# A hybrid encoder layer: input-projection weights split once, stored to DRAM and fetched back for the second half of the tokens

## The chip, the cores and the metric

The kernel runs on one core of one Trainium2 chip. The metric is the device time of one execution in microseconds (us); lower is better.

## The reference, cut to what matters

One layer is computed for 2048 prompt tokens and for 8 sample requests of 16 tokens, which share all weights. Everything is float32.

```python
def layer(x, ...):
    h = rms_norm(x, norm_g[0])
    z = h @ w_in                                   # 1024 -> 3592 columns
    qa, ka, va, qb, kb, vb, ob, ib, fb = split(z)
    att = rms_norm(band_attention(qa, ka, va), g_att)          # 8 heads of 64, band of 9 chunks of 64
    hb = mlstm(qb, kb, vb, ib, fb)                             # 4 heads of 128, state carried along the tokens
    mlstm_out = head_rms_norm(hb) * g_mlstm * sigmoid(ob)
    x = x + rms_norm(concat(att, mlstm_out) @ w_out, norm_g[1])
    x = x + rms_norm(conv_ffn(rms_norm(x, norm_g[2])), norm_g[3])   # 1024 -> 2 x 2816 -> 1024
```

The change concerns `h @ w_in` alone.

## The kernel before, in words

TensorE multiplies in float32r. Each float32 operand is split in two parts, a high part (`h`, a cast on ScalarE) and a low part (`l`, the float32 value less the high part, a subtraction on VectorE), and each product is made of three matmuls (`mm3`, lines 95 to 97: high by high, high by low, low by high).

The tokens are taken in two halves (`HALVES`). In the first are the 8 first tiles of 128 prompt tokens and the sample tile, in the second the 8 last tiles. The columns of `w_in` are cut into 14 groups (`GROUPS`): `va0`, `va1` (values of attention), `qk0` to `qk3` (queries and keys of attention), `qb0` to `qb3` and `vo0` to `vo3` (queries, keys, values and gates of the four mLSTM heads). The list `seq` runs through the 14 groups for the first half and then through the same 14 groups for the second half, so each group's weights are loaded and split twice. A normalised and transposed input (`hT`) of a half stays in SBUF through its 14 groups; `norm_tile` makes it from the rows `xr` (load at line 212, TensorE transposes at line 67 into `hT_pt`).

`load_group` brings the weights of one group, ahead by one group. The tiles `wi_h` and `wi_l` (tags `wh` and `wl`, two buffers each) take the parts. The raw weights come in two pieces `wi_raw` of 512 KB through one buffer (line 1169, issued by SyncE, here SP); each piece is cast and subtracted in two steps (lines 1175 and 1176). The second piece can be loaded only when the first has been split.

Beside the groups run two streams of units, one of attention heads and one of mLSTM heads (`pipes`). `pump` adds up the units' costs of TensorE and VectorE, written in by hand, and takes up to two further units from the streams while VectorE's sum lies below `SHARE` (0.615) of TensorE's. The steps of `load_group` are counted in it: 0.6 us of VectorE for each cast and subtraction. After the last group comes the output projection (`project`, matmuls `wo`), with the rest of the streams beside it, and then the FFN (`ua`, `ub`, `uec`, `dn`, `dnm`).

The order in which the instructions of each engine finally stand is set by a scheduler, which takes the program order as priority and works with its own estimates of durations, so a change in one place moves rows elsewhere. Each engine, SP's list of DMA issues among them, runs its rows strictly in the order that was set. ScalarE (ACT) issues DMAs too: the stores of projected rows (`qTd`, `kTd`, `vd`, `qkbd`, `vobd`). DMA issues also wait, by a semaphore, for earlier DMAs.

Further names in the rows below: `qk_st` is the SBUF copy of a `qk` result (lines 224 and 226) that empties a PSUM bank, of which there are two for these results; `qraw`, `kraw`, `vraw` are attention operands read back; `cs` is the mLSTM state of the samples, `cus` the matmul results on it; `skr`, `svr` are the samples' caches; `whl` is the DRAM tensor that the change adds.

Of the kernel before, what the change touches and what calls it, by code (L numbers as in the profile page):

```python
# [10 lines left out]
F32 = mybir.dt.float32  # L11
F32R = mybir.dt.float32r
# [5 lines left out]
P = 128  # L18
# [26 lines left out]
def hymba_step(ctx: ExitStack, tc: tile.TileContext, I: dict, O: dict):  # L45
    nc = tc.nc

    const = ctx.enter_context(tc.tile_pool(name="const", bufs=1))
    wpool = ctx.enter_context(tc.tile_pool(name="wpool", bufs=1))
    small = ctx.enter_context(tc.tile_pool(name="small", bufs=4))  # L50
    psum = ctx.enter_context(tc.tile_pool(name="psum", bufs=2, space=PSUM))
    dram = ctx.enter_context(tc.tile_pool(name="dram", bufs=1, space=DRAM))
# [10 lines left out]
    def dt_(shape, name):  # L63
        return dram.tile(shape, F32, tag=name, name=name)
# [40 lines left out]
          for p in range(2)]  # L105
    qkbd = [[dt_([P, 2, 512 if s < 4 else 128], f"qkbd{p}_{s}") for s in range(5)] for p in range(4)]
    vobd = [[dt_([P, 4 if s < 4 else 1, 256], f"vobd{p}_{s}") for s in range(5)] for p in range(4)]
    mixd = [dt_([P, 4, D], f"mixd{s}") for s in range(4)]
    mixs = dt_([P, 512], "mixs")
    atts = [dt_([P, 512], f"atts{b}") for b in range(DB)]  # L110
# [131 lines left out]
    def group_T(wh, wl, half, chunks, dsts, scales, name, outs=(None, None)):  # L242
        for c in range(2):
            for ci, tiles in enumerate(HALVES[half]):
                n = len(tiles) * P
                ch = chunks[ci]
                acc = ps_mm(f"{name}_{c}_{ci}")
                for k in range(KT):
                    w = slice(k * 256 + c * P, k * 256 + (c + 1) * P)
                    mm3(acc[:, :n], wh[:, w], wl[:, w], ch[:, 0, k, :n], ch[:, 1, k, :n],  # L250
                        start=(k == 0), stop=(k == KT - 1))
                    if k % 4 == 3:
                        yield n * 12 / 2400, 0.0
                stage = pa.tile([P, 384], F32, tag="st", name=f"{name}_st{c}_{ci}", bufs=2)
                evac_scaled(stage[:, :n], acc[:, :n], scales[c])
                store_T(stage, dsts[c], tiles, outs[c])

    def group_rows(wh, wl, half, chunks, dst, name, width=256, out=None):
        for ci, tiles in enumerate(HALVES[half]):
            for j, t in enumerate(tiles):  # L260
                ch = chunks[ci]
                acc = ps_mm(f"{name}_{t}")
                for k in range(KT):
                    w = slice(k * width, (k + 1) * width)
                    tt = slice(j * P, (j + 1) * P)
                    mm3(acc[:, :width], ch[:, 0, k, tt], ch[:, 1, k, tt], wh[:, w], wl[:, w],
                        start=(k == 0), stop=(k == KT - 1))
                    if k % 4 == 3:
                        yield 1.3, 0.0
                stage = pa.tile([P, 384], F32, tag="st", name=f"{name}_st{t}", bufs=2)  # L270
                evac_scaled(stage[:, :256], acc[:, :256], None)
                if width > 256:
                    nc.vector.tensor_copy(gates[:, gate_ix(t), :], acc[:, 256:width])
                s = 4 if t == SAMPLE else t // 4
                nc.scalar.dma_start(dst[s][:, 0 if s == 4 else t % 4, :], stage[:, :256])
                if out is not None and s >= 3:
                    nc.scalar.dma_start(out[s - 3][:, 0 if s == 4 else t % 4, :], stage[:, :256])
# [536 lines left out]
    def prep(units):  # L814
        yield units
        yield FLUSH
# [338 lines left out]
    SRC = {g: i for i, g in enumerate(["va0", "qk0", "qk1", "va1", "qk2", "qk3",  # L1155
                                       "qb0", "vo0", "qb1", "vo1", "qb2", "vo2", "qb3", "vo3"])}

    def load_group(gi):

        i = SRC[GROUPS[gi]]  # L1160
        src, n = (I["w_in0"], 2112) if i == 0 else (I["w_in1"][i - 1], 2048)
        h = wpool.tile([P, 2112], F32R, tag="wh", name=f"wi{i}_h{gi}", bufs=2)
        l = wpool.tile([P, 2112], F32R, tag="wl", name=f"wi{i}_l{gi}", bufs=2)

        def steps():
            q = n // 2
            for s in range(2):
                raw = pr.tile([P, 1056], F32, tag="wraw", name=f"wi{i}_raw{s}")
                nc.sync.dma_start(raw[:, :q], src[:, s * q:(s + 1) * q])
                yield 0.0, 0.0  # L1170
                yield 0.0, 0.0
                for e in range(2):
                    c = slice(s * q + e * q // 2, s * q + (e + 1) * q // 2)
                    r = raw[:, e * q // 2:(e + 1) * q // 2]
                    nc.scalar.copy(h[:, c], r)
                    nc.vector.tensor_tensor(l[:, c], r, h[:, c], op=ALU.subtract)
                    yield 0.0, 0.6

        return h, l, steps()

    def norm_steps(half):

        for ci, tiles in enumerate(HALVES[half]):
            ch = phT.tile([P, 2, KT, 384], F32R, tag="hT", name=f"hT{half}_{ci}", bufs=3)
            chunks.append(ch)
            for j, t in enumerate(tiles):
                norm_tile(t, ch, j, ps_big)
                yield 0.9, 2.5

    seq = [(half, gi) for half in range(2) for gi in range(14)]  # L1190
# [2 lines left out]
    chunks = []  # L1193
    norms = norm_steps(0)
    next(norms)
    pend = load_group(0)
    for _ in pend[2]:
        pass
    next(norms)
    load_bias()  # L1200
    for n_, (half, gi) in enumerate(seq):
        wh, wl, _ = pend
        split = iter([])
        if n_ + 1 < len(seq):
            pend = load_group(seq[n_ + 1][1])
            split = pend[2]
        g = GROUPS[gi]
        i = int(g[2])
        nm = f"{g}_{half}"
        if g[:2] == "va":  # L1210
            it = group_rows(wh, wl, half, chunks, vd[i], nm, 264 if gi == 0 else 256,
                            [O["v_prompt"][i], O["v_sample"][i].unsqueeze(1)])
        elif g[:2] == "qk":
            it = group_T(wh, wl, half, chunks, [qTd[i], kTd[i]], [-(DA ** -0.5), None], nm,
                         [None, [O["k_prompt"][i], O["k_sample"][i]]])
        elif g[:2] == "qb":
            it = group_T(wh, wl, half, chunks, [[t_[:, c, :] for t_ in qkbd[i]] for c in range(2)],
                         [None, DH ** -0.5], nm)
        else:
            it = group_rows(wh, wl, half, chunks, vobd[i], nm)  # L1220
        if half == 0 and gi == 13:
            chunks = []
            norms = norm_steps(1)
        if n_ == len(seq) - 1:
            out = project([0, 1, 2, 3, 4, 5, 6, 7, SAMPLE, 8, 9, 10, 11, 12, 13, 14, 15])
            split = w_out_steps()
            next(split)
            next(out)
        for u, (pe, dve) in enumerate(it):
            ahead = []  # L1230
            if n_ < len(seq) - 1 or u >= 6:
                ahead.append(next(split, (0.0, 0.0)))
            if n_ == len(seq) - 1 and u == 12:
                ahead.append(next(out))
            if (half == 0 and gi == 13 and u >= 6 and u % 2 == 0) or (gi == 0 and u % 2 == 0):
                ahead.append(next(norms, (0.0, 0.0)))
            pump(pe + sum(a[0] for a in ahead), dve + sum(a[1] for a in ahead))
        for _ in split:
            pass
        if gi == 0:  # L1240
            if half == 0:
                nc.sync.dma_start(bgate, I["b_gate"].broadcast_to([P, 8]))
                nc.sync.dma_start(gatt, I["g_att"])
                heads.append(build_bias)
                mems.append(lambda: prep(prep_sample()))
            mems.append(lambda half=half: prep(prep_prompt(half)))
        if g[:2] == "qk":
            attention(i, half)
            if half == 0 and i == 3:
                heads.insert(len(heads) % 4, lambda: attention_sample(0, EARLY))  # L1250
            if half == 1 and i == 0:
                heads.insert(len(heads) % 4, lambda: attention_sample(EARLY, DB))
        if g[:2] == "vo":
            mems.append(lambda i=i, half=half: mlstm(i, half))
            if half == 0:
                mems.append(lambda i=i: mlstm_sample(i))
# [128 lines left out]
    pend = [load_up(0, 0, 0)]  # L1385
# [17 lines left out]
    for b, tiles in enumerate(FBLOCKS):  # L1403
        last = b == len(FBLOCKS) - 1
        nt = len(tiles)
        n = HALF[b]
# [71 lines left out]
        for f in range(NF):  # L1478
# [7 lines left out]
            e, c = ec[:, 0:512], ec[:, 512:1024]  # L1486
# [33 lines left out]
        pend = pend[0]  # L1520
# [4 lines left out]
        for dh in range(2):  # L1525
# [9 lines left out]
            for c in range(6):  # L1535
                wh, wl = pend
                if c < 5:
                    pend = load_down(dh, c + 1)
                elif dh == 0:
                    pend = load_down(1, 0)  # L1540
                elif not last:
                    quads = [load_quads(b + 1, 0, i) for i in range(2)]
                    pend = [load_up(b + 1, 0, 0, quads[0])]
# [39 lines left out]
            for j in order:  # L1583
                if dh == 0:
                    half, ssq = out[j]
# [3 lines left out]
                else:  # L1589
                    half, ssq = out[j]  # L1590
# [104 lines left out]
```

## Time and profile before

| | |
|---|---|
| time, median of 3 runs (lowest to highest) | 2788.76 us (2788.08 to 2790.21) |
| span of the profiled execution, first to last instruction | 2784.7 us |
| median less span: what lies around the span | 4.1 us |
| busy share of the span: PE, weight loads, DVE, ACT, POOL | 98%, 92%, 67%, 51%, 16% |
| DMA traffic | 486.05 MB, mean 175 GB/s |
| mean granted TensorE clock | 0.998 |

The profile gives no time of its profiled execution other than the span. PE is TensorE, DVE VectorE, ACT ScalarE, POOL GpSimd, SP SyncE. The two halves of the projection take about 0 to 519 us and 519 to 1045 us, the output projection the time to 1313 us, the FFN the rest. In a line of the chain of waits stand the waiting engine with its tile and line, what it waited for, the sum in us, how often, and the longest. In a line of the timeline stand the start, the time taken, the engine, the line, the operation, and in brackets the idle time before it with what ended it.

### The profile page before, as it was taken

Reading aid. Unit: us, or ns where it says so; the run is one execution under the profiler, and the core shown is the slowest. Engines: PE = TensorE matmul, PEld = TensorE weight load, DVE = VectorE, ACT = ScalarE, POOL = GpSimd, SP = SyncE. Lnnn points to the kernel's source line nnn. Section 1 sums busy time; section 2 is a strip of 40 time slices with the busy share of each in tenths; the row PEclk is TensorE's granted clock in tenths of the full one; section 3 lists DMA queues with packets and bytes.
Section 4 is the critical chain, followed back from the end, with each engine's and each line's share of the span. In section 5 each row is a group of like instructions: output and inputs, shape, how many; then the busy total and the mean of one; then the engine's idle time right before and its main releaser. Section 6 shows DMA issues by size and latency. Waiting matters only on the chain.

```text
span 2784.7 us, 47088 instructions
## 1 busy us (share of the span) xinstructions
PE 2723.8 (98%) x16587; PEld 2548.3 (92%) x16587; DVE 1876.3 (67%) x3447; ACT 1409.1 (51%) x2836; POOL 437.4 (16%) x895
## 2 busy tenths in 40 slices
PE   8999999999999999999999999999999999999998
PEld 7899999998899998888999988899999878999887
DVE  5344455656556668666999986457877864888855
ACT  4355555644356666544454555345455543555543
POOL 1000010212000003244111110011111310222220
PEclk9999999999999999999999999999999999999999
DMA  5544355557555555356655455644544774555585
GB/s 185 155 119 136 103 174 162 164 157 217 162 173 148 144 179 171 107 176 227 187 172 167 167 176 174 219 142 153 160 152 141 276 263 152 172 179 180 192 309 190
DMA packets 311883, 486.05 MB, mean 175 GB/s; under 512 B 55426, under 2 KB 150622, under 8 KB 311518
## 3 DMA queue, kind: packets, MB, share of 16 engines
q1 hardware_dynamic: 271134, 442.92, 50.1%
q10 hardware_dynamic: 38592, 33.83, 3.6%
q0 software_dynamic: 1920, 6.29, 0.6%
q8 instruction: 130, 2.13, 0.3%
q14 instruction: 107, 0.88, 0.1%
HBM read 359.36 MB, written 126.70 MB: 175 GB/s over the span
## 4 chain that ended last, share of the span: by engine, by line
PE 55%; DVE 2%; DMA 1%; issue 1%; ACT 1%; POOL 1%; SPq 0%; DVEq 0%; POOLq 0%; ACTq 0%
PE uec L95 6%; PE uec L96 6%; PE uec L97 6%; PE dn L97 4%; PE dn L96 4%; PE dn L95 4%; PE ua L97 3%; PE ua L95 3%; PE ua L96 3%; PE dnm L97 2%; PE dnm L95 2%; PE dnm L96 2%; PE wo L97 2%; PE wo L95 2%; PE wo L96 2%; PE ub L96 1%
## 5 line engine op out<-in xcount | busy, mean ns | idle before, releaser
L95 PE MATMUL uec<-B,wuh 128*128 128x384 f32 (+1 forms) x720 | 234.9, 328 | 2.2 <-DVE uu L1419 1.1
L96 PE MATMUL uec<-B,wuh 128*128 128x384 f32 (+1 forms) x720 | 235.1, 327 | 0.0
L97 PE MATMUL uec<-B,wul 128*128 128x384 f32 (+1 forms) x720 | 233.9, 327 | 0.0
L1266 DVE TENSOR_TENSOR gl<-gr,gh 128x768 fp32r<-128x768 f32 (+3 forms) x141 | 120.4, 863 | 145.8 <-ACT gh L1265 144.5
L1265 ACT CAST gh<-gr 128x768 fp32r<-128x768 f32 (+3 forms) x141 | 102.0, 735 | 200.1 <-PE dn L96 183.2
L1265 ACT CAST wuh<-wu 128x512 fp32r<-128x512 f32 x255 | 141.7, 617 | 112.1 <-PE uec L96 103.2
L95 PE MATMUL dn<-wdh,gh 128*128 128x512 f32 x466 | 182.4, 391 | 2.3 <-DVE ug L1419 2.3
L96 PE MATMUL dn<-wdl,gh 128*128 128x512 f32 x466 | 183.4, 394 | 0.0
L97 PE MATMUL dn<-wdh,gl 128*128 128x512 f32 x466 | 167.9, 396 | 0.0
L1266 DVE TENSOR_TENSOR wul<-wu,wuh 128x512 fp32r<-128x512 f32 x255 | 164.6, 683 | 2.8 <-DMA x2d<-mx 2.8
L393 DVE CUSTOM_DVE_ANT_0 tmp<-s,nb 128x640 f32<-128x640 f32 (+4 forms) x128 | 94.4, 737 | 96.6 <-PE s L383 94.8
L95 PE MATMUL vo<-wi_h,hT 128*128 128x256 f32 x544 | 155.1, 285 | 0.6 <-DVE mt L199 0.6
L97 PE MATMUL vo<-wi_h,hT 128*128 128x256 f32 x544 | 155.6, 286 | 0.0
L96 PE MATMUL vo<-wi_l,hT 128*128 128x256 f32 x544 | 154.8, 285 | 0.0
L95 PEld LDWEIGHTS uec<-B,wuh 128*128 128x128 f32 x720 | 135.0, 188 | 4.2 <-DVE uu L1419 1.6
L95 PE MATMUL qk<-hT,wi_h 128*128 128x384 f32 (+1 forms) x384 | 128.7, 335 | 7.4 <-ACT qk_st L224 6.6
L96 PEld LDWEIGHTS uec<-B,wuh 128*128 128x128 f32 x720 | 135.2, 188 | 0.2
L97 PEld LDWEIGHTS uec<-B,wul 128*128 128x128 f32 x720 | 135.1, 188 | 0.0
L406 DVE TENSOR_TENSOR ptl<-pt,pth 128x640 fp32r<-128x640 f32 (+4 forms) x128 | 93.6, 737 | 57.1 <-ACT pth L405 56.0
L394 ACT ACTIVATE tmp<-tmp,mn 128x640 f32<-128x640 f32 (+4 forms) x128 | 97.6, 762 | 64.6 <-DVE mn L393 61.9
L96 PE MATMUL qb<-hT,wi_h 128*128 128x384 f32 (+1 forms) x384 | 127.8, 333 | 0.0
L96 PE MATMUL qk<-hT,wi_h 128*128 128x384 f32 (+1 forms) x384 | 127.6, 332 | 0.0
(412 smaller groups left out, 8873.0 us busy)
## 6 DMA issues: line engine op xcount, KB each, us to landing
wu<-in_w_up SPq DMA_DIRECT2D x220, 256.0 KB, 4.1
wu<-wsd SPq DMA_DIRECT2D x176, 256.0 KB, 4.2
wdr<-in_w_down SPq DMA_DIRECT2D x132, 256.0 KB, 5.6
gr<-gd SPq DMA_DIRECT2D x78, 384.0 KB, 3.6
wi_raw<-in_w_in SPq DMA_DIRECT2D x52, 512.0 KB, 4.0
wsd<-ws SPq DMA_DIRECT2D x88, 256.0 KB, 2.8
gd<-g SPq DMA_DIRECT2D x44, 384.0 KB, 3.5
kraw<-kTd SPq DMA_DIRECT2D x112, 128.0 KB, 3.2
```

Of the source, the lines that this page charges most:

```text
L95: nc.tensor.matmul(out, ah, bh, start=start, stop=False, skip_group_check=onto)
L96: nc.tensor.matmul(out, ah, bl, start=False, stop=False, skip_group_check=onto)
L97: nc.tensor.matmul(out, al, bh, start=False, stop=stop, skip_group_check=onto)
L393: nc.vector.tensor_tensor_reduce(o_, s_, b_, 1.0, 3e38, ALU.add, ALU.min, accum_out=mn)
L394: nc.scalar.activation(tmp[:, :n], tmp[:, :n], AF.Exp, bias=mn, scale=-1.0, accum_out=rsum[:, i % 4, hh:hh + 1])
L406: nc.vector.tensor_tensor(s.ptl[:, sl, qc], ptv, s.pth[:, sl, qc], op=ALU.subtract)
L1265: nc.scalar.copy(h, r)
L1266: nc.vector.tensor_tensor(l, r, h, op=ALU.subtract)
```

## The change: what it does

In the first half, after both steps of a piece, the high and the low part of that piece are stored from SBUF to a DRAM tensor `whl`, one for each group: four stores of 512 KB a group. In the second half nothing is loaded raw, cast or subtracted; four loads of 512 KB fetch the parts from `whl` straight into `wi_h` and `wi_l`. All 112 new DMAs are issued by SP. The second half's steps are entered in `pump` with a cost of 0.

```diff
+    whl = [dram.tile([P, 2, 2112], F32, tag=f"whl{i}", name=f"whl{i}") for i in range(14)]
...
-    def load_group(gi):
+    def load_group(half, gi):
...
+        def ready():
+            q = n // 2
+            for s in range(2):
+                for x, t in enumerate((h, l)):
+                    nc.sync.dma_start(t.bitcast(F32)[:, s * q:(s + 1) * q], whl[i][:, x, s * q:(s + 1) * q])
+                    yield 0.0, 0.0
+
+        if half:
+            return h, l, ready()
 
         def steps():
             q = n // 2
...
                     nc.scalar.copy(h[:, c], r)
                     nc.vector.tensor_tensor(l[:, c], r, h[:, c], op=ALU.subtract)
                     yield 0.0, 0.6
+                c = slice(s * q, (s + 1) * q)
+                for x, t in enumerate((h, l)):
+                    nc.sync.dma_start(whl[i][:, x, c], t.bitcast(F32)[:, c])
...
-    pend = load_group(0)
+    pend = load_group(0, 0)
...
-            pend = load_group(seq[n_ + 1][1])
+            pend = load_group(*seq[n_ + 1])
```

The scheduler's order changes with it from the start up to the last output projections; from there on it is the same on TensorE. SP's list at the start, before, where the second piece of the weights of `va0` (`wi_raw` of 1056 columns) is loaded:

```order
L1243 DMA gatt<-in_g_att 128x4
L603 DMA mss<-in_state_m 4x8
L491 DMA hgm_0_4089<-in_g_mlstm 128x128
L1169 DMA wi_raw_380<-in_w_in 128x1056
L212 DMA xr_633<-in_x_prompt 128x1024
L298 DMA ext<-reln 8x384
L299 DMA ext<-relf 8x383
```

The same place of SP now, in the fence below (`whl` is the new DRAM tensor, 1056 columns being one piece):

```order
L1257 DMA gatt<-in_g_att 128x4
L604 DMA mss<-in_state_m 4x8
L492 DMA hgm_0_4139<-in_g_mlstm 128x128
L1191 DMA whl_162<-wi_h_386 128x1056
L1191 DMA whl_162<-wi_l_387 128x1056
L1180 DMA wi_raw_396<-in_w_in 128x1056
L213 DMA xr_655<-in_x_prompt 128x1024
L299 DMA ext<-reln 8x384
```

Two stores of the first piece now stand directly ahead of the load of the second.

ScalarE's list in the group `qk0` of the first half, before, from the first evacuation of a key result (`qk_st` from `qk_0_1_0`) on:

```order
L224 COPY qk_0_st_0_1068<-qk_0_1_0_1000 128x384
L239 DMA kTd_0_78<-qk_0_st_0_1068 128x384
L342 COPY qs_0_1290<-qraw_0_1263 128x512
L224 COPY qk_0_st_1_1110<-qk_0_1_1_1071 128x384
L239 DMA kTd_0_78<-qk_0_st_1_1110 128x128
L239 DMA kTd_1_79<-qk_0_st_1_1110 128x256
L1175 COPY wi_h_1165<-wi_raw_1180 128x512 x2
L224 COPY qk_0_st_2_1160<-qk_0_1_2_1114 128x384
```

And the same place of ScalarE's list now:

```order
L225 COPY qk_0_st_0_1092<-qk_0_1_0_1024 128x384
L240 DMA kTd_0_78<-qk_0_st_0_1092 128x384
L225 COPY qk_0_st_1_1136<-qk_0_1_1_1095 128x384
L240 DMA kTd_0_78<-qk_0_st_1_1136 128x128
L240 DMA kTd_1_79<-qk_0_st_1_1136 128x256
L1186 COPY wi_h_1191<-wi_raw_1206 128x512 x2
L225 COPY qk_0_st_2_1186<-qk_0_1_2_1140 128x384
L343 COPY qs_0_1318<-qraw_0_1291 128x512
```

The cast of the attention operand `qraw` has moved behind two more evacuations, and the split of the weights (`wi_h`) stands between them.

SP's list where the second half begins, before; `wi_raw` are the two pieces of the weights of `qk0`, `xr` the input rows of tiles 12 to 15:

```order
L847 DMA skr_3_8019<-in_cache_k 128x512
L212 DMA xr_6992<-in_x_prompt 128x1024
L897 DMA svr_0_8096<-in_cache_v 128x512
L212 DMA xr_7040<-in_x_prompt 128x1024
L668 DMA mqk_6_5719<-qkbd_1_128 128x2x256
L1169 DMA wi_raw_7195<-in_w_in 128x1024
L897 DMA svr_1_8137<-in_cache_v 128x512
L212 DMA xr_7093<-in_x_prompt 128x1024
L735 DMA mbs_5930<-mds 128x128
L1169 DMA wi_raw_7435<-in_w_in 128x1024
L212 DMA xr_7144<-in_x_prompt 128x1024
```

And the same place of SP now, with the four loads of the split weights of `qk0`:

```order
L848 DMA skr_3_8123<-in_cache_k 128x512
L213 DMA xr_7070<-in_x_prompt 128x1024
L898 DMA svr_0_8189<-in_cache_v 128x512
L1170 DMA wi_l_7162<-whl_163 128x1024
L1170 DMA wi_h_7161<-whl_163 128x1024 x2
L1170 DMA wi_l_7162<-whl_163 128x1024
L213 DMA xr_7126<-in_x_prompt 128x1024
L669 DMA mqk_6_5781<-qkbd_1_128 128x2x256
L898 DMA svr_1_8242<-in_cache_v 128x512
L736 DMA mbs_5994<-mds 128x128
L213 DMA xr_7178<-in_x_prompt 128x1024
```

The four loads stand together ahead of the load of the second `xr` of this piece, which stood ahead of the first weight piece before, and they write `wi_h` and `wi_l` themselves, not a buffer of their own.

At the end of the projection the streams stand elsewhere on TensorE: the last attention matmul (`ot`) 615 matmuls before the FFN's first instead of 577, the last mLSTM matmul (`ma`) 444 instead of 803. On VectorE and on ScalarE 56 instructions are fewer in all, on SP 84 DMAs more.

More of the change, by code (lines that the diff above doesn't have):

```diff
@@ L1156, in hymba_step @@
                                        "qb0", "vo0", "qb1", "vo1", "qb2", "vo2", "qb3", "vo3"])}
-    def load_group(gi):
+    def load_group(half, gi):
         i = SRC[GROUPS[gi]]
         src, n = (I["w_in0"], 2112) if i == 0 else (I["w_in1"][i - 1], 2048)
-        h = wpool.tile([P, 2112], F32R, tag="wh", name=f"wi{i}_h{gi}", bufs=2)
-        l = wpool.tile([P, 2112], F32R, tag="wl", name=f"wi{i}_l{gi}", bufs=2)
+        h = wpool.tile([P, 2112], F32R, tag="wh", name=f"wi{i}_h{half}", bufs=2)
+        l = wpool.tile([P, 2112], F32R, tag="wl", name=f"wi{i}_l{half}", bufs=2)
+        def ready():
[6 more added lines that the diff above has]
+            return h, l, ready()
         def steps():
```

## The prediction

> **What bounds the kernel now.** I read the page first: span, busy shares, the slices of DMA traffic and the DMA issues.
>
> ```profile
> span 2784.7 us, 47088 instructions
> PE 2723.8 (98%) x16587; PEld 2548.3 (92%) x16587; DVE 1876.3 (67%) x3447; ACT 1409.1 (51%) x2836; POOL 437.4 (16%) x895
> GB/s 185 155 119 136 103 174 162 164 157 217 162 173 148 144 179 171 107 176 227 187 172 167 167 176 174 219 142 153 160 152 141 276 263 152 172 179 180 192 309 190
> wi_raw<-in_w_in SPq DMA_DIRECT2D x52, 512.0 KB, 4.0
> x2d<-mx SPq DMA_DIRECT2D x17, 512.0 KB, 2.6
> ```
>
> PE is busy for 98% and no other engine for more than 67% (weight loads run beside the matmuls). The change removes no matmul, so it can win only PE's idle time, and lose wherever it makes PE idle. The second view is the table by stage; its columns are each engine's busy us (instructions), granted clock, DMA share, GB/s.
>
> ```profile
> core 0: us, PE busy (x) PEld busy (x) DVE busy (x) ACT busy (x) POOL busy (x), PEclk, DMA share, GB/s
> 0.00:120.00 120.00, 99.66 (x640) 95.31 (x641) 52.34 (x133) 46.75 (x92) 12.07 (x40) 0.99 0.58 177
> 120.00:528.00 408.00, 407.25 (x2966) 401.72 (x2964) 212.15 (x476) 216.91 (x508) 24.76 (x75) 1.00 0.47 140
> 528.00:770.00 242.00, 229.04 (x1552) 214.36 (x1553) 134.68 (x394) 106.02 (x274) 40.69 (x120) 1.00 0.58 178
> 770.00:1036.00 266.00, 266.00 (x2076) 264.19 (x2075) 165.19 (x381) 166.94 (x402) 16.23 (x51) 1.00 0.53 157
> 1036.00:1313.00 277.00, 270.24 (x1473) 227.30 (x1472) 198.91 (x318) 138.19 (x330) 100.13 (x137) 1.00 0.51 166
> 1313.00:2784.70 1471.70, 1451.64 (x7887) 1345.47 (x7885) 1113.07 (x1749) 734.27 (x1230) 243.47 (x474) 1.00 0.57 188
> ```
>
> Stage less PE's busy time is PE's idle time: 20.3 us in the first 120; 0.7 in the rest of the first half; 13.0 from 528 to 770; 0.0 from 770 to 1036; 6.8 in the output projection; 20.1 in the FFN, whose order the change leaves alone. All that the removed casts could give back lies in the 13.0 and the 6.8. Third, what PE waits for in the first of these (sum, times, longest):
>
> ```profile
> PE cus L781 <- DMA cs<-in_state_c: 5.0, 6, 2.0
> PE ss L95 <- ACT skh L852: 1.7, 2, 1.5
> PE hT_pt L67 <- DVE xr L219: 1.2, 1, 1.2
> PE cus L781 <- DVE nums L783: 1.2, 1, 1.2
> PE ms L686 <- DVE num L704: 0.8, 1, 0.8
> PE ms L686 <- DVE w L692: 0.5, 1, 0.5
> PE ma L698 <- DVE num L704: 0.5, 2, 0.3
> PE ss L96 <- DVE skl L853: 0.4, 1, 0.4
> ```
>
> None is a wait for projection weights. ACT and DVE end 6.3 us of it (the last seven rows), and one DMA, the samples' state, ends 5.0.
>
> **Part by part.** Each part ends with the value taken and its two ends, in us of PE's idle time; a plus is slower.
>
> *The second piece of va0 (start).* It now stands behind two stores of 512 KB. The page's store of that size lands in 2.6 us, so at worst it is 2 x 2.6 = 5.2 later; but another wait has PE at the start:
>
> ```profile
> PE hT_pt L67 <- DVE xr L219: 8.7, 2, 8.2
> ```
>
> This is PE waiting for its first input rows, 8.2 us at once, and it covers most of the delay. Taken: +1.0 (0 to +5.2).
>
> *40 to 120 us.* ACT's and PE's timeline show how a DMA reaches PE in the first half:
>
> ```profile
> 60.64 0.49 ACT L226 ACTIVATE qk_st<-qk 128x384 f32<-128x384 f32 x1 [1.45 <-PE qk L97]
> 64.88 0.49 ACT L226 ACTIVATE qk_st<-qk 128x384 f32<-128x384 f32 x1 [0.92 <-PE qk L97]
> ...
> 81.98 0.62 ACT L342 CAST qs<-qraw 128x512 fp32r<-128x512 f32 x1 [10.99 <-DMA qraw<-qTd]
> ...
> 108.02 0.48 ACT L224 COPY qk_st<-qk 128x384 f32<-128x384 f32 x1 [7.30 <-DMA qTd<-qk_st]
> ...
> 83.03 0.45 PE L95 MATMUL qk<-hT,wi_h 128*128 128x384 f32 x1 [3.24 <-ACT qk_st L224]
> ...
> 108.55 0.69 PE L95 MATMUL qk<-hT,wi_h 128*128 128x384 f32 x1 [3.34 <-ACT qk_st L224]
> ```
>
> ACT sat 10.99 us on a DMA; the evacuation queued behind that cast came late, both PSUM banks were full, and PE stalled 3.24. At 108 the same happened with 7.30 and 3.34. Evacuations are 4.2 us apart (60.64 to 64.88): an ACT wait shorter than that is covered by the second bank, a longer one shows on PE. In the new order the cast of `qraw` stands behind two more evacuations, which should end the first stall, -3.2; three groups' stores now run through these queues, and I put one new stall of the second kind against it, +3.3. Taken: +0.1 (-6.6, both go, to +6.6, two more come).
>
> *The rest of the first half.* SP's list has two stores directly ahead of every raw load. They wait for the split of the same piece, as the raw load did before:
>
> ```profile
> SPq L1169 <- DVE wi_l L1176: 52.6, 26, 9.1
> ACT wi_h L1175 <- DMA wi_raw<-in_w_in: 10.5, 9, 2.3
> ```
>
> The first row (to 1120 us) is SP waiting for the split, as it will go on doing; no other row of SP waits longer for that than now. The second (120 to 528) is ACT waiting for a raw piece, nine times, 1.2 us each, harmless because under 4.2. What is new is the transfer: 1.05 MB of stores, issued just ahead. At the highest rate of any slice, 309 GB/s, they take 3.4 us, and their two issues 2 x 0.33 (the issue time of a load, in a row below), together 4.1. A wait of 1.2 becomes 5.3, 1.1 above what the second bank covers; nine of them are 9.9. At the low end the reordering moves the casts back far enough, 0. I take four of the nine: +4.4 (0 to +9.9). This is the largest term, and the one I know least.
>
> *The half boundary.* Timelines of PE and SP:
>
> ```profile
> 519.16 0.28 PE L95 MATMUL va<-wi_h,hT 128*128 128x264 f32 x1
> ...
> 521.20 0.33 SPq L212 DMA_DIRECT2D xr<-in_x_prompt  x1
> ...
> 526.87 1.04 PE L67 MATMUL hT_pt<-ident,xr 128*128 128x128 f32 x8
> ...
> 538.14 1.06 PE L67 MATMUL hT_pt<-ident,xr 128*128 128x128 f32 x8 [1.20 <-DVE xr L219]
> ```
>
> The second half's first matmul starts at 519.16, when the first half's last weights come free; only then can the four loads of `qk0` be issued, and now they stand ahead of the `xr` issued at 521.20, which the transposes use from 526.87 on. The issue itself hardly moves; the 2.1 MB ahead of it do. At 309 GB/s they take 6.8 us; one after the other at the raw load's 4.0 they take 16.0. In the new order 39 more matmuls stand ahead of that transpose: at 407.25 / 2966 = 0.137 us each, 5.4 us of cover. So 6.8 - 5.4 = +1.4 is taken (0, if they overlap within 5.4, to 16.0 - 5.4 = +10.6).
>
> By the Trainium skill, "DMA: Bandwidth & Descriptors", section "Bandwidth", 1 MB takes 6.15 us; an estimate from it for the four loads is 12.3, this term would be +6.9, and the time 5.5 above my forecast. No run here shows such a burst; the slice at 309 GB/s speaks for the lower value.
>
> *528 to 770, casts.* The casts in the second half:
>
> ```profile
> L1175 ACT CAST wi_h<-wi_raw x52: 601/618/640, 522.0 to 973.2; 128x512 fp32r<-128x512 f32 x52
> L1176 DVE TENSOR_TENSOR wi_l<-wi_raw,wi_h x52: 680/685/892, 522.6 to 974.5; 128x512 fp32r<-128x512 f32 x52
> L1176 DVE TENSOR_TENSOR wi_l<-wi_raw,wi_h x26: 680/686/892, 530.4 to 753.9; 128x512 fp32r<-128x512 f32 x26
> ```
>
> Half of the 52 lie in this stage. 26 x 0.686 = 17.8 us of DVE's 134.7, 13%, and 26 x 0.618 = 16.1 of ACT's 106.0, 15%, go. PE's 6.3 us behind ACT and DVE are chains that end on their latency; with 13 to 15% less in front of them I take a quarter off: -1.5 (-6.3 to 0).
>
> *528 to 770, loads.* Each of the six groups loaded here brings four loads at once, 6.8 us at 309 GB/s where one raw piece took 4.0: 2.8 more for a small load that falls behind them. `cs` is already late by 0.8 on average, so a delay of it shows in full. I take one sixth of 2.8 for each group, 6 x 0.5 = +3.0 (0 to 6 x 2.0 = +12, 2.0 being the longest of today's waits).
>
> *770 to 1036.* The other 26 casts run beside a PE that idles 0.0, so their removal is worth 0; the loads have no wait of PE here to lengthen. Taken: 0.
>
> *Output projection.* Nothing is removed here, but the mLSTM stream ends 359 matmuls later than before, so its chains have longer to run beside `wo`, whose weights hold DVE at 198.9 of 277 us. It can take away the 6.8 us of idle time or double it; I take -1.0 (-6.8 to +6.8).
>
> Sum: 1.0 + 0.1 + 4.4 + 1.4 - 1.5 + 3.0 + 0 - 1.0 = +7.4. The profiled span of 2784.7 becomes 2792.1; the median of the runs, 4.1 above the span, goes from 2788.8 to **2796.2**, 0.27% slower. A change below 0.2%, 5.6 us, can hardly be told from none on this kernel.
>
> **The rivals.** *All transfers are hidden.* For it: DMA is busy for only 0.47 to 0.58 of a stage, and in 120 to 528 PE lost 0.7 us although ACT waited nine times. Against it: the stores do not spread out, they stand in a bunch ahead of the load that ACT waits for. Then the terms 4.4 and 3.0 fall away: +0.0, 2788.8.
>
> *Faster: the casts were what held the second half.* DVE is then the engine that the chains of attention and mLSTM share, and without the splits all 6.3 us go, with half of the output projection's 6.8 and only the +1.0 at the start to pay: -8.7, 2780.1. For it: seven of the eight rows above name ACT or DVE. Against it: each is short (1.5 at most) and stands behind a chain, and none names a weight cast. It decides if PE's waits for ACT and DVE from 528 to 770 fall below about 2 us.
>
> *Slower still: bunched loads.* If four loads together take longer than about 8.0 us, twice the raw piece's 4.0, what stands behind them in the queues comes too late each time: `cs` costs 12 instead of 3.0, and the stores cost their upper 9.9 instead of 4.4. The sum is 7.4 + 9.0 + 5.5 = +21.9, 2810.7. For it: `cs` is already late. Against it: the highest slice, 309 GB/s, moves 2.1 MB in 6.8. The Trainium skill, "DMA: Bandwidth & Descriptors", section "Issuing engines are not separate DMA queues", says that DMAs of all engines run on the same 16 DMA engines and interleave; by that ACT's stores and small loads would share the delay, as the 7.30 at 108 suggests.
>
> *The change does not do what it says.* Excluded: the new order has 56 casts and 56 subtractions fewer and 84 DMAs more on SP.
>
> **How the numbers follow.** The forecast gets 0.36, transfers hidden 0.28, casts the bound 0.24, bunched loads 0.12. Slower by over 0.2% is the forecast with the last, 0.48; within 0.2%, 0.28; faster, 0.24. Cases of both signs hold most of the chance: the forecast's own range is 2794.4 (0.2%) to 2803.6 (7.4 more: half of the 5.5 and the 9.2 that the stores and the boundary have left above the values taken). The range for 8 in 10 is 2779 to 2808: about 0.1 of the faster case lies below, if a stall of the first 120 us goes too, and 0.1 of the bunched loads above.
>
> **What would show each step.** PE's idle time by stage: 0.7 should become 4 to 6 in 120 to 528, with `qk`, `va` or `qb` waiting for ACT, and ACT for `wi_raw`, some 5 us each; if it stays below 1.5, that term was wrong. From 528 to 770 the waits for ACT and DVE should fall to about 5 and those for `cs` rise to about 8. At the boundary a transpose should wait for `xr` for some 1 to 3 us. The issue-to-landing time of the `whl` loads, four together, decides for or against the bunched loads: under 7 us against, over 8 for. The forecast is wrong if the median is below 2790, or if the loss lies in the FFN, where the order is the same.

## The result, and the profile after

The changed kernel takes 2822.52 us (median of 4 runs, 2815.90 to 2831.18) against 2789.35 for the kernel before: 1.0120 of its time, 95% interval 1.0098 to 1.0141. It is slower, as forecast, but by 33 us where 7.4 were forecast, and above the range. A second set of runs of the same kernel gave 1.0116 (1.0095 to 1.0138).

The profiled execution took 44.8 us longer than that of before; it was the slowest of its four runs, 8.7 us above their median, and the one of before seems to lie below its own. (The time of each run of the changed kernel is 1.7 us above its span; if the same holds before, only 1.7 of the 4.1 us between span and median lie around the span, and its profiled execution took, as an estimate, 2786.4.) So the parts below add up to more than the difference of the medians. The page, and the core's span and mean clock:

```profile
span 2829.5 us, 47079 instructions
PE 2747.0 (97%) x16587; PEld 2566.3 (91%) x16587; DVE 1841.4 (65%) x3391; ACT 1378.8 (49%) x2780; POOL 440.0 (16%) x895
wi_raw<-in_w_in SPq DMA_DIRECT2D x26, 512.0 KB, 6.2
core 0: 2829.5 us, clock 0.990
```

The same 16587 matmuls keep PE busy for 23.2 us longer (2747.0 against 2723.8), and PE idles for 21.6 us longer. The first comes with the granted clock, 0.990 now and 0.998 before.

Since the work moves, the stages are cut at the same points of the program: the first `qk` matmul, the first `va` of the second half, the first `wo`, the first `ua`. Before:

```profile
0.00:48.40 48.40, 35.44 (x267) 33.90 (x268) 28.78 (x45) 26.75 (x44) 9.99 (x33) 1.00 0.60 199
48.40:519.20 470.80, 462.77 (x3269) 454.66 (x3268) 228.97 (x554) 230.00 (x539) 25.91 (x79) 1.00 0.47 140
519.20:1045.80 526.60, 511.77 (x3762) 494.42 (x3761) 314.65 (x804) 287.20 (x713) 58.98 (x176) 1.00 0.57 171
1045.80:1313.50 267.70, 262.71 (x1414) 220.30 (x1413) 191.36 (x300) 130.86 (x312) 99.01 (x133) 1.00 0.50 164
1313.50:2784.70 1471.20, 1451.14 (x7885) 1345.07 (x7883) 1112.57 (x1748) 734.27 (x1230) 243.47 (x474) 1.00 0.57 188
```

And after:

```profile
0.00:56.30 56.30, 37.60 (x267) 35.80 (x268) 29.51 (x45) 27.07 (x44) 10.71 (x33) 0.95 0.71 247
56.30:533.40 477.10, 466.19 (x3267) 456.51 (x3267) 225.76 (x549) 226.41 (x535) 24.43 (x79) 0.99 0.62 193
533.40:1070.90 537.50, 517.46 (x3719) 498.67 (x3718) 275.70 (x727) 254.69 (x639) 54.54 (x170) 0.98 0.62 191
1070.90:1359.20 288.30, 274.26 (x1456) 229.98 (x1456) 195.57 (x324) 136.33 (x334) 103.88 (x140) 0.98 0.47 155
1359.20:2829.50 1470.30, 1451.47 (x7885) 1345.29 (x7883) 1114.81 (x1749) 734.32 (x1230) 246.43 (x474) 1.00 0.57 188
```

The second column is the length: +7.9 at the start, +6.3 in the rest of the first half, +10.9 in the second half, +20.6 in the output projection, -0.9 in the FFN. DVE lost 39 us of work in the second half (314.65 to 275.70) and PE got nothing for it. 43 of its matmuls moved from there to the output projection, so those two stages are best read as a sum, +31.5.

**The clock.** The table over one stall in the output projection of the changed kernel:

```profile
1180.00:1183.50 3.50, 0.88 (x5) 0.46 (x4) 2.99 (x4) 0.99 (x4) 2.99 (x3) 1.00 0.00 0
1183.50:1187.50 4.00, 3.37 (x17) 3.01 (x18) 3.51 (x10) 2.12 (x5) 0.00 (x0) 0.54 0.43 126
1187.50:1191.00 3.50, 3.50 (x16) 3.32 (x16) 0.95 (x3) 1.60 (x3) 1.73 (x5) 0.55 0.39 133
1191.00:1200.00 9.00, 9.00 (x45) 7.40 (x44) 4.66 (x10) 3.89 (x10) 0.02 (x1) 1.00 0.53 155
```

PE works 0.88 of 3.5 us, and then the clock is near half for 7 us of almost full work. In the trace's clock records the half-speed stretches come in pieces of 3.4 us: 6.8 us in all before, 54.6 after (the one that runs into the end of the span left out). Half of the difference, 23.9, is the 23.2 us by which PE is busy longer. PE's stalls of 2 us or more, the first 15 us left out, went from 2 to 9. So a stall of 2 us that such a stretch follows costs another 1.7 or 3.4 us when it is over; 8 of the 9 were followed by one.

The Trainium skill, "TensorE: Matmul & The Clock Gate", section "HAM oscillation — how this bites in real kernels", puts it as a rule against idle gaps above about 3.4 us and charges half of the throttled time. The traces agree on the half; on the threshold they differ: counted over the 13 profiles of this case, after the first 60 us, a half-speed stretch stood at or just behind 30 of 45 stalls of 2.0 to 2.5 us and 12 of 141 of 0.8 to 1.5 us.

### The profile page after: what moved, and what is told of

Its sections match the earlier page's. It is cut to its first block, busy times and chain, and to the rows that moved or that the text cites. A ratio compares the mean times of both kernels' runs of the same rounds, so it can differ in the third digit from the quotient of the medians.

```text
span 2829.5 us, 47079 instructions
## 1 busy us (share of the span) xinstructions
PE 2747.0 (97%) x16587; PEld 2566.3 (91%) x16587; DVE 1841.4 (65%) x3391; ACT 1378.8 (49%) x2780; POOL 440.0 (16%) x895
## 4 chain that ended last, share of the span: by engine, by line
PE 52%; DVE 3%; DMA 2%; issue 1%; POOL 1%; ACT 1%; SPq 0%; DVEq 0%; POOLq 0%; ACTq 0%
PE uec L95 6%; PE uec L96 6%; PE uec L97 6%; PE dn L97 4%; PE dn L96 4%; PE dn L95 3%; PE ua L97 3%; PE ua L96 3%; PE ua L95 3%; PE dnm L97 2%; PE dnm L95 2%; PE dnm L96 2%; PE ub L96 1%; PE ub L95 1%; PE ub L97 1%; PE wo L95 1%
## 5 line engine op out<-in xcount | busy, mean ns | idle before, releaser
L97 PE MATMUL qk<-hT,wi_l 128*128 128x384 f32 (+1 forms) x384 | 129.4, 337 | 0.0
```

The source lines that it names most:

```text
L97: nc.tensor.matmul(out, al, bh, start=False, stop=stop, skip_group_check=onto)
```

## The experiments

Two theories to begin with: the stores and loads hold up what stands behind them (stores S, loads L), or the order of the units, which the cost of 0 in `pump` changes, costs the time (O). The ratios are against the runs of before on the same chip. The stage lengths are of one profiled execution each and all set against the one profile of before; the FFN, whose order no run changes, takes 1469.2 to 1473.7 us in them, so a stage difference of 2 or 3 us shows little by itself.

**Stores only.** `ready()` is not used; `whl` is written in the first half and never read.

```diff
-        if half:
-            return h, l, ready()
...
+                if half == 0:
                     for x, t in enumerate((h, l)):
                         nc.sync.dma_start(whl[i][:, x, c], ...)
```

> The first half stores the split parts as the change does, the second half loads, casts and subtracts as before; whl is written and never read. In the profiled run of the change the loss was 14 us up to the half boundary, 12 in the second half of the projection, 20 in the output projection, -1 in the FFN. Theory S (stores delay rows and operands in SP's list and in the queues): the first 14 us stay, the rest goes, about 2803. Theory O (all but little of the loss comes from the order of the units, which the cost of 0 in pump makes): 2789 to 2793. If the stores cost nothing, 2789.

Measured 2801.38, ratio 1.0049 (1.0034 to 1.0064). Its table, cut at the same points:

```profile
0.00:54.50 54.50, 36.73 (x266) 35.03 (x267) 29.39 (x45) 26.92 (x44) 10.77 (x33) 0.97 0.73 255
54.50:532.40 477.90, 466.35 (x3267) 456.47 (x3267) 227.83 (x553) 228.95 (x539) 25.89 (x79) 0.99 0.61 191
532.40:1061.50 529.10, 512.97 (x3762) 495.72 (x3761) 314.33 (x806) 287.59 (x714) 57.72 (x177) 1.00 0.56 170
1061.50:1330.90 269.40, 264.13 (x1414) 221.32 (x1413) 188.06 (x298) 130.51 (x311) 100.08 (x133) 0.99 0.49 162
```

+6.1 and +7.1 in the first half, as in the change; 2.5 and 1.7 behind it. Theory S holds for the first half, and the output projection's 20 us are not the stores'. A stall of this kernel, in its timeline, shows the way from DMA to PE:

```profile
476.47 0.43 SPq L672 DMA_DIRECT2D mvo<-vobd  x1
478.58 0.42 ACT L649 ACTIVATE mvo<-mvo 128x256 f32<-128x256 f32 x1 [4.25 <-DMA mvo<-vobd]
478.90 0.81 ACT L395 ACTIVATE tmp<-tmp,mn 128x640 f32<-128x640 f32 x1
479.86 0.77 PE L67 MATMUL pt<-ident,tmp 128*128 128x128 f32 x5 [1.26 <-ACT tmp L395]
```

ACT sits 4.25 us on an operand, `tmp` stands behind it in ACT's list, and PE waits for `tmp`. It was an operand of the mLSTM stream, not a weight; at the same place before, ACT waited 0.55 us. No store of `whl` stands near it in SP's list, so which transfer delayed it is not shown.

**Loads only.** Stores of one group alone, four loads a group in the second half.

```diff
+                if i == 7:
...
-    whl[i][:, x, s * q:(s + 1) * q]
+    whl[7][:, x, s * (2048 - q):s * (2048 - q) + q]
```

> The second half fetches wi_h and wi_l with four loads a group as the change does, and the steps cost 0 in pump; but the first half stores only the parts of one group (vo0), and every load of the second half reads these, so the second half multiplies by wrong weights. From the last 10400 rows on TensorE's order is that of the change. Theory O (order) and theory L (bunched loads) both expect the losses of the second half and the output projection here, 20 to 31 us, 2809 to 2820, and the first half as before (half boundary at 519 to 521). Theory S expects little: about 2792.

Measured 2804.46, ratio 1.0059 (1.0044 to 1.0074), a little below the range expected. Second half and output projection:

```profile
520.10:1043.80 523.70, 509.81 (x3719) 492.44 (x3718) 275.69 (x723) 255.87 (x638) 53.90 (x169) 0.99 0.62 195
1043.80:1330.80 287.00, 273.71 (x1457) 229.87 (x1457) 195.27 (x326) 136.12 (x334) 103.41 (x140) 0.98 0.49 157
```

-2.9 and +19.3: the loss of the output projection is all here without the stores, and the second half's is not. Loads and order were still changed together; the next two kernels part them.

**The change with the cost kept.**

```diff
                 for x, t in enumerate((h, l)):
                     nc.sync.dma_start(..., whl[i][:, x, s * q:(s + 1) * q])
                     yield 0.0, 0.0
+                yield 0.0, 0.6
+                yield 0.0, 0.6
```

> The change as it is, but the steps of the second half are entered in pump with 0.6 of VectorE, as many and in the same places as before, so that the units come in the program order of before. Theory O: the 20 us in the output projection and most of the 12 before it go, about 2803 (the stores' 14 stay). Theory L (the loads themselves delay the second half): stays at 2815 to 2822.

Measured 2806.51, ratio 1.0063 (1.0048 to 1.0078).

```profile
534.80:1064.00 529.20, 515.54 (x3764) 498.40 (x3762) 281.26 (x751) 260.88 (x661) 56.09 (x176) 0.99 0.62 196
1064.00:1333.60 269.60, 264.13 (x1410) 221.42 (x1411) 191.22 (x300) 131.23 (x312) 98.83 (x134) 0.99 0.49 162
```

+2.6 and +1.9 instead of +10.9 and +20.6, with the same loads and stores: theory O for the output projection, and theory L fails as the cause of much.

**The kernel before with the cost 0.** The casts are all made.

```diff
-                    yield 0.0, 0.6
+                    yield 0.0, 0.0 if half else 0.6
```

> The kernel before, with loads, casts and subtractions in both halves and no whl; only the cost of the second half's casts in pump is 0 instead of 0.6. Theory O: the output projection and the end of the second half lose as in the change, 15 to 25 us, 2804 to 2814, more than in the change if the casts that are still made also hurt. Theories S and L: 2789, no difference.

Measured 2804.28, ratio 1.0052 (1.0037 to 1.0067).

```profile
519.60:1050.40 530.80, 511.60 (x3718) 493.40 (x3717) 307.02 (x776) 279.95 (x689) 54.18 (x169) 0.99 0.56 167
1050.40:1333.50 283.10, 271.91 (x1458) 226.96 (x1457) 198.67 (x328) 137.06 (x336) 102.06 (x140) 0.99 0.48 159
```

+4.2 and +15.4 from one number in a planner and not one DMA more. So the cost of 0 is shown from both sides: put into the kernel before, it makes most of the loss of the output projection; taken out of the change, it ends it.

**The change again.** 

> The change itself once more, for a second profile beside kernels that differ from it in one thing. The profiled run before was the slowest of four (2831 against a median of 2823). What belongs to the change should repeat: some 6 to 9 us to the first qk matmul, 13 to 15 to the half boundary, 15 to 21 in the output projection. If the 11 us between the boundary and the output projection are stalls that come and go, they are clearly smaller here.

Ratio 1.0116 as above; the profiled span was 2828.3. To the first `qk` +6.4, to the half boundary +14.3, from there to the first `wo` +7.9, output projection +19.6. The parts repeat, the second half's a little smaller.

**First three groups left as they were.** With the cost kept, `va0`, `qk0` and `qk1` are neither stored nor fetched (`i > 2` in both conditions).

> The change with the cost of 0.6 kept in pump (as in the run with the cost kept, 2806.5), and the first three groups (va0, qk0, qk1) not stored in the first half and split again in the second. Theory: the stores of the first 60 us delay the sample's input rows by 8 us. Then the first qk matmul is back at 48 to 50 us and the time 6 to 9 lower than 2806.5, about 2799. If the start was lost for another reason, 2804 to 2808.

Measured 2801.45, ratio 1.0037 (1.0025 to 1.0048), the first `qk` at 49.5 us. The start is the stores', as expected; the rest of the first half, 478.6 us against 470.8, is not mended (16 matmuls more lie in it, about 2 us).

**Stores issued by GpSimd.** With the cost kept, `nc.gpsimd.dma_start` for the stores.

> The change with the cost of 0.6 kept, and the 56 stores issued by GpSimd instead of SP. Same bytes, but SP's list no longer has stores, that wait for the split, ahead of loads. If the place in SP's list is what costs the first half, it loses 0 to 4 us there instead of 15, about 2793 to 2797. If it is the traffic itself (1 MB of stores ahead of each load in the 16 DMA engines), 12 or more, about 2804 to 2808.

Measured 2802.54, ratio 1.0042 (1.0028 to 1.0055). Table of the first half, and the raw loads' issue to landing:

```profile
0.00:49.80 49.80, 35.59 (x266) 33.81 (x267) 29.20 (x45) 27.22 (x44) 16.62 (x41) 1.00 0.81 279
49.80:529.10 479.30, 467.81 (x3283) 456.17 (x3282) 227.95 (x555) 228.06 (x538) 50.21 (x127) 1.00 0.63 194
wi_raw<-in_w_in SPq DMA_DIRECT2D x26, 512.0 KB, 6.6
```

An answer between the two that I had offered: the start is back with the same traffic, so it was the place in SP's list; the rest of the first half is not (+8.5), and the raw loads take 6.6 us as against 4.0 before, with no store in their queue. That leaves the traffic as the likely cause, but does not show it: 14 matmuls more lie in that stretch, about 2 us, and GpSimd now waits for the casts ahead of its stores (162.5 us in all), so its other work may have come later. By the Trainium skill, "DMA: Bandwidth & Descriptors", section "Issuing engines are not separate DMA queues", DMAs of all engines run on the same 16 DMA engines whoever issues them; the 6.6 agrees.

**Loads spread out.** With the cost kept, a load only at every second unit, and the 0.6 entered beside each load instead of behind two.

> The change with the cost of 0.6 kept, and one load every second unit instead of one every unit, so that the four loads of a group do not stand together in SP's list. If bunched loads hold up small loads behind them, the 6 us lost between the first qb of the second half and the output projection (305.4 against 299.1) fall to 0 to 3, about 2801 to 2803. If not, 2806.

Measured 2821.98, ratio 1.0104 (1.0080 to 1.0128): wrong. The second half took 539.8 us (+13.2), the output projection 276.1 (+8.4). The cost now fell on other units, and the order changed with it, so the run does not tell what bunched loads cost. It may be a second case of theory O; nothing here parts the two.

**One source.** The change, row for row in the same order, with all stores; the loads read `whl[7]` alone, as in the loads-only kernel.

> The change itself, in the same order on every engine, with all its stores; only the loads of the second half all read the parts of one group (2 MB of whl) instead of those of 14 (29 MB), so the second half multiplies by wrong weights. In two profiles of the change the projection's second half lost 11 and 8 us against before; with loads but without most stores and from one group's parts it gained 3. If the place that is read makes the difference, the gain is back here: second half -3 to 0, time 2813 to 2817. If not, +8 to +11 and 2822 to 2825, and the loss comes from where the stores have put the transfers.

Measured 2824.83, ratio 1.0112 (1.0095 to 1.0128). Second half 532.1 us (+5.5), output projection 287.4 (+19.7). The second half lies between the two answers expected, the time at the second: where the parts are read from makes no difference to the time.

**Loads only, cost kept.** The loads-only kernel with the two 0.6 of the third experiment.

> Loads in the second half without casts, the cost of 0.6 kept in pump, stores of one group only (all loads read these, so the second half multiplies by wrong weights). This is what the idea is worth without the price of the stores and with the order of the units as before. If the casts held PE, the second half gains 3 to 7 us and the time is 0.1 to 0.3% below the kernel before. If the removed casts lay beside PE and the loads cost as much as they save, within 2 us of it.

Measured 2797.72 against 2794.57, ratio 1.0011 (1.0001 to 1.0020).

```profile
521.20:1050.90 529.70, 515.70 (x3763) 498.65 (x3761) 279.97 (x747) 261.09 (x660) 55.02 (x175) 0.99 0.62 195
1050.90:1323.10 272.20, 264.24 (x1410) 221.29 (x1411) 191.27 (x301) 131.42 (x312) 98.93 (x134) 0.99 0.49 160
```

The idea's whole worth, its stores not paid for and its order as before: nothing, or a loss of 0.1%. DVE does 280 us instead of 315 in the second half, and the stage is not shorter: 3.1 longer in this profile, whose span is 11.5 longer than that of before, where the medians differ by 3.15.

**Four groups only.** `va1`, `qk2`, `qk3`, `qb0`, stores by GpSimd, cost kept.

> Only the groups va1, qk2, qk3 and qb0 are stored and fetched split, the stores issued by GpSimd, the cost of 0.6 kept. These are the groups whose casts lie in the stage where PE waited for ACT and DVE, and no store falls into the first 80 us. If stores and order are the whole price, it is paid for four groups of 14 only: first half +1 to +3, second half -3 to 0, about the time of before (0.998 to 1.002). If it is 6 us or more slower, a cost is missing in my account.

Measured 2811.13, ratio 1.0072 (1.0047 to 1.0098): wrong, and a cost was missing in my account.

```profile
1055.30:1349.00 293.70, 279.35 (x1472) 232.52 (x1471) 201.84 (x329) 141.96 (x340) 99.06 (x141) 0.98 0.49 158
```

The output projection is 26.0 us longer, with 1472 matmuls in it instead of 1414, and this with the cost kept. (The profiled execution is the slowest of four, 12 us above their median.) `pump` takes the units here as before, by its code, so the cost of 0 is one way into a bad order, not the only one: here the scheduler made one by itself.

No version was faster than the kernel before, and the loads-only kernel with the cost kept speaks against any large gain from leaving out the casts.

## Why the prediction was wrong

The ratios add up: stores 0.49%, cost of 0 0.52%, loads without casts 0.11%, together 1.12% against 1.20 and 1.16 measured. Two of them at a time fit as well: stores and loads 0.60 (0.63 measured with the cost kept), loads and cost 0.63 (0.59, loads only). By the prediction's own steps:

*Output projection, -1.0 (-6.8 to +6.8): this step failed.* It measured +20.6, outside both ends: PE's idle time there went from 5.0 to 14.0 us, two half-speed stretches of 6.8 us cost about 6.8 more, and the rest goes with the 42 matmuls that moved in, 24 `ma` and 18 `ms`. The prediction saw the mLSTM stream end 359 matmuls later and took it for room; it is the opposite. The cost of 0 in `pump`, which moved these units, had no term. The waits of PE in that stage, after (1070 to 1360):

```profile
PE mT_pt L67 <- DVE mr L986: 7.2, 5, 2.6
PE h2T_pt L1094 <- DVE x2r L1086: 1.6, 1, 1.6
```

and the largest one before (1045 to 1314):

```profile
PE pt L67 <- DVE ptl L406: 1.8, 1, 1.8
```

`mr` are the rows that the output projection reads back and multiplies, and PE waited for none before. The longest of the five waits:

```profile
1177.82 0.63 ACT L984 ACTIVATE mt<-mr 128x512 fp32r<-128x512 f32 x1
1180.81 2.55 DVE L986 TENSOR_SCALAR mr<-mr,att_rs 128x512 f32<-128x512 f32 x1 [0.51 <-POOL att_rs L84]
1183.42 0.79 PE L67 MATMUL mT_pt<-ident,mr 128*128 128x128 f32 x4 [2.62 <-DVE mr L986]
```

The rows were not late: their load was issued at 1163.76, and ACT begins on them without waiting. Two small steps of POOL and the DVE step follow, and the DVE step takes as long before (2.6 us in the median of both kernels). What is missing is other work for PE in these 5.6 us. In the program's order fewer than half as many attention units are left for the output projection, since a VectorE sum without the casts lets `pump` take more of them earlier; in the profile the last `ot` stands 638 matmuls ahead of the FFN's first (not 615, as said above), against 577 before. The four kernels with 96 `ma` matmuls or 144 `ot` in that stage instead of 72 and 132 (the change, loads only, cost 0, four groups) take 283 to 294 us there; six others 267 to 272, the spread loads 276; the two repeats of the change's order (again, one source) take 287. PE's wait for `mr` stands in each of the kernels with 276 us or more (2.3 to 8.8 us) and in none of the six. That it is the missing work beside `wo` is read from these rows, not tested by itself.

*The clock was left out.* Every term priced a stall at its own length; most stalls of 2 us and more cost the half-speed stretch too, about 23 us of the 44.8. The prediction had a row for it (PEclk) and no term.

*The second piece of va0, +1.0 (0 to +5.2)* measured +7.9 and +6.4. The cover that was named, the wait for the first input rows, lies before the stores. What came late is the last rows of the half. SP, ACT and PE after:

```profile
39.03 1.20 SPq L1180 DMA_DIRECT2D wi_raw<-in_w_in  x1
41.44 0.33 SPq L213 DMA_DIRECT2D xr<-in_x_sample  x1
49.84 1.06 ACT L217 ACTIVATE hT<-xr 128x1024 fp32r<-128x1024 f32 x1 [3.63 <-DMA xr<-in_x_sample]
53.27 1.31 PE L67 MATMUL hT_pt<-ident,xr 128*128 128x128 f32 x8 [4.58 <-DVE xr L220]
```

and the same load and its reader before:

```profile
36.39 0.33 SPq L212 DMA_DIRECT2D xr<-in_x_sample  x1
41.22 1.06 ACT L216 ACTIVATE hT<-xr 128x1024 fp32r<-128x1024 f32 x1 [3.81 <-DMA xr<-in_x_sample]
```

The sample rows' load was issued 5.1 us later, behind eight stores, landed 8.6 later, and PE stood still.

*40 to 120 us, +0.1, and the rest of the first half, +4.4*: +6.3 measured for both, within the bounds. The size was near; the mechanism was not the one named: the raw loads did slow from 4.0 to 6.2 us, but ACT's waits for `wi_raw` from 120 to 528 did not grow (9.6 us in seven, 10.5 in nine before). PE idled 6.5 us there instead of 0.7, but in no `qk`, `va` or `qb`: its waits were for ACT's `tmp`, behind casts that waited 7.39 us for `kraw` and 4.74 for `mvo`.

*Half boundary, +1.4*: within its ends, near the low one. From the first `va` to the first `qk` of the second half it lost 0.1 and 1.0 in the two profiles of the change.

*Casts, -1.5, and loads, +3.0, from 528 to 770; nothing behind it.* With the order as before the second half lost 2.6 (cost kept) and 3.1 (loads only, cost kept), which can't be told from the +1.5 forecast; that is in part luck, since `cs`, which was to rise from 5.0 to about 8, stayed at 4.4 us in both the change and the kernel with the cost kept. In the change the second half lost 10.9 and 7.9, and part of that lies behind 770, where the prediction saw no wait of PE to lengthen:

```profile
768.49 0.46 SPq L1170 DMA_DIRECT2D wi_h<-whl  x1
769.27 0.33 SPq L1170 DMA_DIRECT2D wi_l<-whl  x1
769.65 0.60 SPq L1170 DMA_DIRECT2D wi_h<-whl  x1
770.30 0.99 SPq L1170 DMA_DIRECT2D wi_l<-whl  x1
771.39 0.50 SPq L848 DMA_DIRECT2D skr<-in_cache_k  x1
779.65 0.63 ACT L853 CAST skh<-skr 128x528 fp32r<-128x528 f32 x1 [8.08 <-DMA skr<-in_cache_k]
780.33 0.39 PE L95 MATMUL ss<-skh,zhl 128*128 128x264 f32 x1 [2.25 <-ACT skh L853]
```

Four loads, a small load behind them, ACT waiting 8.08 us for it, PE 2.25, and then 6.8 us at half speed. That is the rival of bunched loads, in one place. The sign that was named speaks against it on the whole, 6.5 and 6.7 us from issue to landing in the median, under the 7:

```profile
wi_l<-whl SPq DMA_DIRECT2D x26, 512.0 KB, 6.5
wi_h<-whl SPq DMA_DIRECT2D x26, 512.0 KB, 6.7
```

Why the second half loses 5 to 11 us in the change and gains 2.9 in the loads-only kernel stays open. It is not the place that is read (one source). It may be order: TensorE's rows in the loads-only kernel are those of the change only from the middle of the group `qb1` of that half on. The spread loads did not answer it.

*The rivals.* Hidden transfers fall with the stores alone, 0.49%. Faster was out of reach: loads only with the cost kept gave 1.0011. Bunched loads as a whole were priced at +21.9 and came nearest to the 33 measured, by luck: most of the loss has other causes.

## What to carry to other kernels

A number in a planner's cost table is part of the change: look for it in the diff, and try it alone before the rest, since here 0.6 set to 0 cost as much as 29 MB of stores. Price a stall of TensorE of about 2 us at more than its length: here the clock halved behind two in three of them and cost another 1.7 us or more. Work taken off an engine that TensorE hardly waited for was worth nothing here, whatever its share of the engine's time; and what replaced it on the DMA queues was not free, though these were busy for only 47% to 60% of the time.

## What the runs showed of the hardware that I had not expected

The half clock set in behind most stalls of 2.0 to 2.5 us (30 of 45 in the 13 profiles) and lasted 3.4 us or a multiple of it, 10.2 at most. Stores of 29 MB spread over the first half (56 of 512 KB; the traffic there went from 140 to 193 GB/s) raised a 512 KB load beside them from 4.0 to 6.2 us, and to 6.6 when another engine issued them.
